# A hybrid token-mixing and expert layer on one core: a written TensorE and ScalarE order up to the end of the u projection

## The chip, the cores and the metric

The kernel runs on one core of one Trainium2 chip. The metric is the device time of one execution in microseconds (us); less is better. A core has TensorE (PE, matrix products; its weight loads are listed as PEld), VectorE (DVE), ScalarE (ACT), GpSimd (POOL) and SyncE (SP), which issues most DMA transfers. Each engine works through its own list of instructions in order, and waits for the others by semaphores.

## The reference

One layer for 512 latent tokens and 256 context tokens, 1024 wide, in float32:

```
mod   = silu(c) @ ada_w + ada_b            # 6 vectors of 1024; the same for c_ctx
h, hc = modulate(rms_norm(x)), modulate(rms_norm(ctx))      # shift 1 and scale 1
q, k, v, r, lr, u = split(h @ w_in)                         # the same for hc
GLA:  log_a = log_sigmoid(lr @ lr_up + bias) / 16; a gated linear scan in both directions
S5:   lam_bar = exp(lam*dt); b_bar = ((lam_bar-1)/lam)*B; a diagonal complex scan of u, both directions
x  = x + g1 * (concat(GLA, S5) @ w_out)
x  = x + g2 * moe(modulate(rms_norm(x)))   # 32 experts, 4 for each token
out = rms_norm(x)
```

## The kernel before, in words

Everything lies in one function, `hybrid_layer_kernel`, and in `moe_phase`, which it calls at the end. The Python code issues operations; a scheduler decides each engine's list from its own model of time, except inside `manual_schedule` blocks, where the named engines keep the order in which the code stands. Tiles come from rings of named slots, and a tile waits until a slot of its ring is free. Those that matter here:

- `place(n)` are 13 single slots of 1 MB; `half(n)` are six of 512 KB, which first hold the six tiles `xt` of x and ctx.
- `whalf(name)` without a number is a ring of three 512 KB slots. It carries t32s, then the four tiles of `wu` (weights of u), the first tile of `wqk` (weights of q and k), the tile vt0, the other three of `wqk`, qT, kT and then `wv` and `wr_`.
- `work(...)` is a ring of four slots of 256 KB, called t2k. It carries, in the order of the code, the scratch of the S5 weights (`wtmp`, L399), the scratch of the output weights (`cd`, L441, also named wtmp in the trace), the copies of u (uT and uTc, L622 to L630), two rows mb (L503) and the temporaries of the gates (ab, abc).
- `bank` is a ring of six PSUM banks, `side` gives one of two more.

The order of the work up to the end of u. SP has a written list of early loads (L166 to L183): four tiles of x, eight of `ada_w` for the first half of the features, `wu`, ctx, B, `wu`, eight more of `ada_w`, C. `turned_tokens` (L229) scales and transposes a tile of tokens; ScalarE's order of this is written (L245). `shifts(p, k)` (L267) multiplies one tile of `ada_w`, `columns(p)` (L276) makes the scale and shift columns A1, B1 from it, and `modulate(p)` (L518) applies them, p being the half of the features. The first half stands before u. For S5, `pick` and two blocks of transposes (L331 to L373) spread the decays and B, and `chunk_weights(d)` (L391) forms for each direction d eight blocks with three VectorE operations, a block of transposes and a ScalarE copy each.

The u projection is 32 units (L577 to L594), four slices h of the features by eight outputs; a unit is two matrix products. TensorE's order of it is written: eight `shifts(1, k)`, `columns(1)` after unit 4, `low_rank` before unit 17 and a step of `condition` (L486) after every second unit from unit 9 (units count from 0). A step of `condition` reads 1 MB of `ada_w` into a ring of two slots and multiplies it; there are 16, for the four other modulation vectors. After the loop, and outside of the written order, stand `chunk_weights(0)` and `(1)`, `output_columns` (L411: the C columns cc), `output_weights` (L424: 16 groups of three VectorE operations for cl), the VectorE work of the long decays lv, the copies of u to DRAM and back, the remaining steps of `condition` and its end. Then follow the gates (L672 to L691), `lags` (L446, reads cl), the projection of q and k (pk, L732 to L739, with `chunk_inputs` after its first slice, which fills vt and XV for the scan), the scan on VectorE, and the projections v (pvv) and r (pr), attention, output projection, norm, router, and the 32 experts, each with 12 MB of weights.

Of the kernel before, what the change touches and what calls it, by code (L numbers as in the profile page):

```python
# [20 lines left out]
D = 1024  # L21
L = 512
# [16 lines left out]
AFTER = (1, 2, 3, 4)  # L39
LOW0 = 7  # L40
LOW1 = 17
COND0 = 9
COND = 2
# [7 lines left out]
def hybrid_layer_kernel(ctx, tc, I, out, tap=None, stage=99):  # L51
# [114 lines left out]
    with tc.manual_schedule(engines={mybir.EngineType.SP}):  # L166
# [13 lines left out]
        for r, cn in enumerate(("s5_c_re", "s5_c_im")):  # L180
            for d in range(2):
                nc.sync.dma_start(crow[r][d * 16:(d + 1) * 16].rearrange("q h c p -> q h (c p)"),
                                  I[cn][0, d].rearrange("(h q) c p -> q h (c p)", h=2))  # L183

    pr = bank("ps_rows")
# [4 lines left out]
    nc.scalar.activation(sg, cols[:, 0:16], AF.Exp, scale=-1.0)  # L190
    V.tensor_scalar(sg, sg, 1.0, None, OP.add)
    V.reciprocal(sg, sg)
    stc = consts.tile([P, KT, 32], F32, name="stc")
    nc.gpsimd.memset(stc, 0.0)
    for j in range(2):
        nc.vector.tensor_tensor(stc[:, :, j], cols[:, 8 * j:8 + 8 * j], sg[:, 8 * j:8 * j + 8], op=OP.mult)
# [26 lines left out]
    def squares(i):  # L223
        sq = work("sq", (P, D), BF)
        ss = small.tile([P, 1], F32, name="ss")
        nc.scalar.activation(sq, xt[i], AF.Square, accum_out=ss)
        return rstd_root(nc, small, ss, D)

    def turned_tokens(i, root):  # L229
        t = xt[i]  # L230
        rs = rstd_inv(nc, small, *root)
        V.tensor_scalar(t, t, rs, None, OP.mult)
        for hh in range(2):
            pb = bank(f"xT{i}{hh}")
# [10 lines left out]
    with tc.manual_schedule(engines={mybir.EngineType.Activation}):  # L245
        decays()
        root = squares(0)
        for i in range(4):
            after = squares(i + 1) if i < 3 else None
            turned_tokens(i, root)  # L250
            root = after
        angles()
        for i in range(4, 6):
            turned_tokens(i, squares(i))

    gates_w = half(0, "gates_w", (P, 768))
    lrs = gates_w[:, 0:256].rearrange("p (k r) -> p k r", k=KT)
    nc.sync.dma_start(lrs, win[:, :, 1536:1568])  # L260
    gw = gates_w[:, 256:768].rearrange("p (z n) -> p z n", z=2)
    nc.gpsimd.memset(gw, 0.0)
    gnw = consts.tile([P, P], F32, name="gnw")
# [3 lines left out]
    def shifts(p, k):  # L267
        if k == 0:
            pa.append(side(f"ps_ada{p}", 0) if p else bank(f"ps_ada{p}"))
        for c in range(2):  # L270
            for hh in range(2):
                q = 2 * c + hh
                nc.tensor.matmul(pa[p][32 * q:32 * q + 32, :256], stc[:, k, :], adac[p][k][:, c, hh * 256:(hh + 1) * 256],
                                 start=(k == 0), stop=(k == KT - 1), skip_group_check=True)

    def columns(p):  # L276
        with tc.high_priority():
            mrow = work("mrow", (P, 256))
            nc.vector.tensor_copy(mrow, pa[p][:, :256])
            pm = side("ps_mod", 0) if p else bank("ps_mod")  # L280
            for b in range(2):
                transpose(pm[:, b * P:(b + 1) * P], mrow[:, b * P:(b + 1) * P])
            pmv = pm[:, :256].rearrange("p (b c h j) -> p c h b j", b=2, c=2, h=2)
# [6 lines left out]
            for j in range(2):  # L290
                a_, b_ = [o[p][:, j].rearrange("p (h b) -> p h b", h=2) for o in (A1, B1)]
                nc.vector.scalar_tensor_tensor(a_, pmv[:, 1, :, :, j], 1.0, col(24), op0=OP.add, op1=OP.add)
                nc.vector.tensor_tensor(a_, a_, col(32), op=OP.mult)
                nc.vector.tensor_tensor(b_, pmv[:, 0, :, :, j], col(16), op=OP.add)

    for k in range(KT):
        shifts(0, k)
    columns(0)
# [3 lines left out]
    for g2 in range(2):  # L302
        nc.gpsimd.dma_start(rows2[0:4].rearrange("t (q g c) -> t g q c", q=4, g=2)[:, g2],
                            I["s5_d"][0, g2 * 256:(g2 + 1) * 256].rearrange("(t q c) -> t q c", t=4, q=4))
    nc.gpsimd.dma_start(rows2[4:8], I["gla_lr_bias"].rearrange("o z (r p) -> (o z r) p", p=P))
    nc.gpsimd.dma_start(rows2[8:12], I["glu_b"].rearrange("o (r p) -> (o r) p", p=P))
    pr2 = side("ps_pq", 1)
    transpose(pr2[:, :NR2], rows2, NR2)
    V.tensor_copy(cols[:, NR:], pr2[:, :NR2])

    lb = [t32("lbr"), t32("lbi")]
    ff = [t32("ffr"), t32("ffi")]
    V.tensor_tensor(sh, sh, sh, op=OP.mult)
    V.tensor_scalar(sh, sh, -2.0, 1.0, OP.mult, OP.add)
    V.tensor_tensor(lb[0], ea, sh, op=OP.mult)
    V.tensor_tensor(lb[1], ea, sn, op=OP.mult)
    den, t0 = t32("den"), t32("t0")
    V.tensor_tensor(den, lamr, lamr, op=OP.mult)
    V.tensor_tensor(t0, lami, lami, op=OP.mult)
    V.tensor_tensor(den, den, t0, op=OP.add)  # L320
    V.reciprocal(den, den)
    V.tensor_scalar(nn, lb[0], -1.0, None, OP.add)
    V.tensor_tensor(ff[0], nn, lamr, op=OP.mult)
    V.tensor_tensor(t0, lb[1], lami, op=OP.mult)
    V.tensor_tensor(ff[0], ff[0], t0, op=OP.add)
    V.tensor_tensor(ff[0], ff[0], den, op=OP.mult)
    V.tensor_tensor(ff[1], lb[1], lamr, op=OP.mult)
    V.tensor_tensor(t0, nn, lami, op=OP.mult)
    V.tensor_tensor(ff[1], ff[1], t0, op=OP.subtract)
    V.tensor_tensor(ff[1], ff[1], den, op=OP.mult)  # L330
    def pick(ps, src):  # L331

        for g2 in range(2):
            sel = ident[:64, :64].rearrange("k (d g n) -> k g d n", d=2, g=2)[:, g2]
            nc.tensor.matmul(ps[g2 * 64:(g2 + 1) * 64], src, sel, start=True, stop=True, skip_group_check=True)

    pq = side("ps_pq", 1)
    for i, t in enumerate(lb + ff):
        pick(pq[:, i * 32:(i + 1) * 32], t)

# [4 lines left out]
    V.tensor_copy(pw[:, :, 1], pq[:, 0:64].rearrange("p (r g) -> p r g", r=2))  # L345
    V.tensor_copy(fz, pq[:, 64:128].rearrange("p (r g) -> p r g", r=2))
# [10 lines left out]
    for n in (1, 2, 4):  # L357
        bb = [pw[:, r, n:n + 1].to_broadcast([P, n, 32]) for r in range(2)]
        cmul(V, [pw[:, r, n + 1:2 * n + 1] for r in range(2)], [pw[:, r, 1:n + 1] for r in range(2)], bb,
             ctmp[:, :n * 32].rearrange("p (k g) -> p k g", g=32))  # L360

    bb_ = [consts.tile([P, 32, 16], F32, name=f"bb{r}") for r in range(2)]
    pb_ = []
    for r in range(2):
# [7 lines left out]
    fb = [fz[:, r].rearrange("p (g o) -> p g o", o=1).to_broadcast([P, 32, 16]) for r in range(2)]  # L372
    cmul(V, bb_, pb_, fb, ctmp.rearrange("p (g c) -> p g c", c=16))  # L373
# [17 lines left out]
    def chunk_weights(d):  # L391
        pr_, pi_ = powers(0, d, d == 1, 0, True), powers(1, d, d == 1, 0, True)
        br_, bi_ = over_powers(bb_[0], d, True), over_powers(bb_[1], d, True)
        wr = [place(3 + 4 * d + r, f"w{'ri'[r]}{d}", (P, 16, 16, 8)) for r in range(2)]
        wt[d] = [place(5 + 4 * d + r, f"wt{d}{r}", (P, 16, P)) for r in range(2)]
        for g in range(0, 16, 4):
            gs = slice(g, g + 4)
            for r, (o, a, b, op) in enumerate(((wr[0], pr_, pi_, OP.subtract), (wr[1], pi_, pr_, OP.add))):
# [4 lines left out]
                pb = side("ps_w", 1)  # L403
                for j in range(4):
                    transpose(pb[:, j * P:(j + 1) * P], o[:, g + j].rearrange("p c k -> p (c k)"))
                nc.scalar.activation(wt[d][r][:, gs].rearrange("p g s -> p (g s)"), pb, AF.Copy)
# [17 lines left out]
    def output_weights():  # L424
        for r in range(2):
            bd.append(whalf(f"bd{r}", (P, 32, 32), n=3 + r))
            nc.gpsimd.memset(bd[r], 0.0)
# [58 lines left out]
    def condition():  # L486
        ring = keep_.tile([P, 2, 2048], F32, name="adb2", tag="xv")
        mob = whalf("mob", (P, 2, 512), n=5)

        def step(g, k):  # L490
            if k == 0:
                pa2.append(side(f"pa2{g}", 0))
            t = ring[:, k % 2]
            nc.sync.dma_start(t, I["ada_w"][0, k * P:(k + 1) * P, 2048 + g * 2048:4096 + g * 2048])
            for q in range(4):
                nc.tensor.matmul(pa2[g][32 * q:32 * q + 32, :], stc[:, k, :], t[:, q * 512:(q + 1) * 512],
# [21 lines left out]
    def modulate(p):  # L518
        with tc.high_priority():
            for kk in range(4):  # L520
                for m, n, src in sides(p):
                    h, a, b = src[:, kk], A1[p][:, m, kk:kk + 1], B1[p][:, m, kk:kk + 1]
                    if (kk + m) % 2:
                        last = nc.scalar.activation(h, h, AF.Identity, bias=b, scale=a)
                    else:
                        V.tensor_scalar(h, h, a, b, OP.mult, OP.add)
        return last
# [9 lines left out]

    modulate(0)
# [35 lines left out]
    ahead["wu", 2] = wcols("wu", 1568, 2)  # L574
    cond, cond_end = condition()
    todo_c = [(g, k) for g in range(2) for k in range(KT)]
    with tc.manual_schedule(engines={mybir.EngineType.PE}):  # L577
        late = list(range(4, KT))
        for k in range(4):
            shifts(1, k)  # L580
        for i, (h, o) in enumerate([(h, o) for h in range(4) for o in (outs if h else outs[0::2] + outs[1::2])]):
            if i == LOW0:
                ahead["wu", 3] = wcols("wu", 1568, 3)
            if i == LOW1:
                low_rank()
            unit(ahead["wu", h][0], h, *o)
            if i >= COND0 and (i - COND0) % COND == 0:
                cond(*todo_c.pop(0))
            if late and i in AFTER:
                shifts(1, late.pop(0))  # L590
                if not late:
                    columns(1)
                    last = modulate(1)
    with tc.issue_after(last.ins):  # L594
# [1310 lines left out]
```

## Time and profile before

| | us |
|---|---|
| median of 3 runs (1537.7 to 1538.61) | 1538.43 |
| the profiled execution, its whole time | 1538.63 |
| span of its trace, first to last instruction | 1536.8 |
| TensorE busy in the span | 1348.4 (88%) |
| VectorE busy | 530.0 (34%) |
| ScalarE busy | 250.5 (16%) |
| GpSimd busy | 169.0 (11%) |

Times within the profile count from the start of the span. The whole time is 1.8 us longer than the span. Busy time of TensorE overlaps from one matrix product to the next, and its ends are modelled, so it is read as occupancy. In a timeline, a row gives start, length, engine, line, operation and operands; in brackets stands how long the engine had been idle before and what ended that.

### The profile page before, as it was taken

The numbers are of one execution on the slowest core, as the hardware profiler recorded it, in microseconds if no ns is written. First come the engines' busy times: TensorE is split into PE (matmuls) and PEld (weight loads), VectorE is DVE, ScalarE is ACT, GpSimd is POOL, SyncE is SP. The second block draws the span as 40 slices with busy tenths as digits, with TensorE's granted clock in tenths as the row PEclk, the third lists the DMA queues.
The fourth block names the chain that finished last, engine by engine and source line by source line (L and its number), as shares of the span: only waits on it lengthen the run. The fifth ranks groups of instructions, "written<-read, shape, count | busy, mean of one in ns | idle before, by whom it ended". The sixth has DMA issues, their size and how long they took to land. (4 is left out here: it accounts for less than half of the span.)

```text
span 1536.8 us, 21011 instructions
## 1 busy us (share of the span) xinstructions
PE 1348.4 (88%) x8122; PEld 546.3 (36%) x8122; DVE 530.0 (34%) x1378; ACT 250.5 (16%) x548; POOL 169.0 (11%) x159
## 2 busy tenths in 40 slices
PE   3796577999796899999999999999999888888985
PEld 2443253458443233333332333332333222222322
DVE  5952737946337113113212221111221122212125
ACT  4112451144222001001000010000010010000013
POOL 2000000000001001121111121111111111111110
PEclk9898698999898999999999999999999999999998
DMA  9474324223725999999999999999999999999993
GB/s 313 138 243 155 84 82 110 68 67 110 281 105 208 393 368 404 409 410 414 411 406 412 415 409 415 404 414 409 414 411 405 408 415 410 410 404 410 413 400 121
DMA packets 104907, 487.18 MB, mean 317 GB/s; under 512 B 24062, under 2 KB 30878, under 8 KB 53584
## 3 DMA queue, kind: packets, MB, share of 16 engines
q1 hardware_dynamic: 89072, 456.95, 74.6%
q0 software_dynamic: 13984, 24.94, 6.0%
q10 hardware_dynamic: 1728, 3.56, 0.6%
q8 instruction: 88, 1.44, 0.4%
q14 instruction: 35, 0.29, 0.1%
HBM read 468.41 MB, written 22.86 MB: 320 GB/s over the span
## 5 line engine op out<-in xcount | busy, mean ns | idle before, releaser
L1568 PE MATMUL pg<-gu,xT 128*64 128x512 f32 x2048 | 480.6, 601 | 34.7 <-DMA gu<-in_exp_w_gu_dram 27.9
L1568 PEld LDWEIGHTS pg<-gu,xT 128*64 128x64 f32 x2048 | 138.8, 137 | 330.5 <-issue 242.4
L1601 PE MATMUL pd<-dn,aT 128*64 128x512 f32 x992 | 222.8, 594 | 12.0 <-DMA dn<-in_exp_w_down_dram 9.6
L1588 DVE TENSOR_SCALAR at<-rest 128x256 f32<-128x256 f32 x32 | 13.6, 425 | 555.9 <-PE rest L1581 307.2
L1589 ACT ACTIVATE sgm<-at 128x256 f32<-128x256 f32 x96 | 39.7, 413 | 700.7 <-DVE at L1588 677.2
L1601 PEld LDWEIGHTS pd<-dn,aT 128*64 128x64 f32 x992 | 68.5, 136 | 145.5 <-issue 113.0
L1536 POOL DMA_INDIRECT xg<-h2d,iu x47 | 50.1, 1065 | 588.1 <-DVE li L1590 328.7
L1581 PE MATMUL rest<-gu,xT 128*32 128x512 f32 x896 | 107.3, 597 | 0.0
L1652 POOL DMA_INDIRECT acc<-y,iu x30 | 47.7, 1589 | 205.0 <-DMA acc<-yr,iu 175.0
L1552 ACT ACTIVATE aT<-turn 128x512 f32<-128x512 f32 x64 | 27.9, 487 | 204.0 <-PE turn L114 204.0
L1652 POOL DMA_INDIRECT acc<-yr,iu x30 | 48.2, 1607 | 56.7 <-DMA acc<-y,iu 32.7
L1650 DVE SCALAR_TENSOR_TENSOR yr<-rest,gt,g2r 128x256 f32<-128x256 f32 x30 | 14.5, 483 | 107.9 <-DMA acc<-yr,iu 73.7
L1611 PE MATMUL rest<-dn,aT 128*32 128x256 f32 x896 | 50.8, 379 | 0.0
L1581 PEld LDWEIGHTS rest<-gu,xT 128*32 128x32 f32 x896 | 24.4, 109 | 69.1 <-issue 67.9
L114 PE MATMUL turn<-ident,at 128*128 128x128 f32 x192 | 32.0, 302 | 9.3 <-PEq L1686 4.7
L549 PE MATMUL pvv<-wv_w,xn 128*128 128x512 f32 x64 | 31.2, 645 | 7.2 <-DMA wv_w<-in_w_in_dram 7.2
L1592 DVE TENSOR_TENSOR at<-at,sgm 128x256 f32<-128x256 f32 x96 | 37.3, 415 | 0.0
L1591 DVE SCALAR_TENSOR_TENSOR at<-li,at 128x256 f32<-128x256 f32 x96 | 37.2, 414 | 0.0
L1450 DVE CAST e<-mt 96x64 bf16<-96x64 f32 x32 | 6.3, 206 | 89.3 <-PEq L1686 46.3
L114 PEld LDWEIGHTS turn<-ident,at 128*128 128x128 f32 x192 | 25.8, 209 | 30.1 <-issue 25.7
L1498 DVE TENSOR_TENSOR ohs<-mt 128x1024 bf16<-128x1024 f32 x30 | 36.5, 1215 | 0.0
L549 PE MATMUL pk<-xn,wqk_w 128*128 128x512 f32 x64 | 31.5, 629 | 3.1 <-DVE la L683 3.1
(550 smaller groups left out, 1429.1 us busy)
## 6 DMA issues: line engine op xcount, KB each, us to landing
gu<-in_exp_w_gu_dram SPq DMA_DIRECT2D x252, 1024.0 KB
dn<-in_exp_w_down_dram SPq DMA_DIRECT2D x128, 1024.0 KB
adb<-in_ada_w_dram SPq DMA_DIRECT2D x16, 1024.0 KB
ada<-in_ada_w_dram SPq DMA_DIRECT2D x16, 512.0 KB
wo<-in_w_out_dram SPq DMA_DIRECT2D x4, 1024.0 KB
gu<-in_exp_w_gu_dram POOLq DMA_DIRECT2D x4, 1024.0 KB, 11.7
xt<-in_x_dram SPq DMA_DIRECT2D x4, 512.0 KB
wu_w<-in_w_in_dram SPq DMA_DIRECT2D x4, 512.0 KB
```

The lines of the kernel that those rows point to most:

```text
L114: nc.tensor.transpose(ps, src, ident[:k, :k])
L549: nc.tensor.matmul(o, lhs(k, w[:, kk]), rhs(k, w[:, kk]), start=opens and k == 0, stop=k == KT - 1, skip_group_check=True)
L1498: V.tensor_tensor(ohs, iot.rearrange("p (o s) r -> p o (s r)", o=1).to_broadcast([P, 4, 2 * P]), pm.to_broadcast([P, 4, 2 * P]), op=OP.is_ ...
L1536: last = nc.gpsimd.indirect_dma_start(out=x[:, c0:c1], out_offset=None, in_=src, in_offset=bass.IndirectOffsetOnAxis(ap=iu[:, s:s + 1], ax ...
L1568: nc.tensor.matmul(pg[b][64 * q:64 * q + 64], xT[:, k % 4, (k // 4) * 64:(k // 4 + 1) * 64], gu[k][:, :, c:c + 256], start=False, stop=(k ...
L1581: nc.tensor.matmul(pr[32 * q:32 * q + 32], xT[:, 4 + k % 2, (k // 2) * 32:(k // 2 + 1) * 32], gu[k][:, :, q * 256:(q + 1) * 256], start=Fa ...
L1589: nc.scalar.activation(sg, at, AF.Sigmoid, scale=1.702)
L1591: V.scalar_tensor_tensor(at, li, 1.0, at, op0=OP.add, op1=OP.mult)
L1592: V.tensor_tensor(at, at, sg, op=OP.mult)
L1601: nc.tensor.matmul(pd[64 * q:64 * q + 64], aT[:, k % 4, (k // 4) * 64:(k // 4 + 1) * 64], dn[k][:, q * 512:(q + 1) * 512], start=False, st ...
L1611: nc.tensor.matmul(pe[32 * q:32 * q + 32, 0:256], aT[:, 4 + k % 2, (k // 2) * 32:(k // 2 + 1) * 32], dn[k][:, q * 256:(q + 1) * 256], star ...
L1652: nc.gpsimd.indirect_dma_start(out=dst, out_offset=bass.IndirectOffsetOnAxis(ap=iu[:, s:s + 1], axis=0), in_=src, in_offset=None, bounds_c ...
```

## The change

From the start up to the last unit of u, both TensorE and ScalarE now keep a written order. In it:

- the squares of a token tile, its scaling and its transposes are separate functions that are called one tile ahead of each other; the eight `shifts(0, k)` stand between them; the units on the latent tokens of slice 0 begin when the first half of the latent features is modulated, and the two context tiles, the S5 pieces (`small_columns`, `picked`, `input_rows`) and the context's modulation stand between the first units;
- `shifts(1, k)` come two at a time after units 7 to 10; `columns(1)` then uses ScalarE for its PSUM copies and GpSimd for its six small operations, and `modulate(1)` is all on ScalarE;
- a step of `condition` follows every unit from 12 until the 16 are done; its ring has four places of 1 MB (two of them in the slots that held x and ctx tiles), filled by two DMAs each;
- the transposes and copies of `chunk_weights` become 16 turns, one after every unit from 14; `low_rank` moves to unit 20, `output_columns` into the loop at unit 23; the VectorE part of `chunk_weights(1)` and the long decays are issued at unit 10;
- `output_weights` moves behind the copies of u in the code; three small loads (gnw, rwt, rbb) move from GpSimd's queue to the end of SP's early list; two memsets of bd and one each of gw and stc move from GpSimd to VectorE;
- vt0, vt1, qT and kT leave the ring `whalf` for slots of their own (whalf 5 and 4, place 10).

The core of the diff:

```
+ADA1 = (7, 8, 9, 10)
+LOW = 20
+OUT = 23
+COND0 = 12
+CHUNK0 = 14
...
+        nc.sync.dma_start(gnw, raw(I["gla_norm_w"], 0, [[0, P], [1, P]]))
+        nc.sync.dma_start(rwt, I["router_w"][0].rearrange("(k p) e -> p k e", p=P))
+        nc.sync.dma_start(rbb, raw(I["router_b"], 0, [[0, P], [1, 32]]))
...
     def columns(p):
+        eng = nc.gpsimd if p else V
         with tc.high_priority():
             mrow = work("mrow", (P, 256))
-            nc.vector.tensor_copy(mrow, pa[p][:, :256])
+            if p:
+                nc.scalar.activation(mrow, pa[p][:, :256], AF.Copy)
+            else:
+                V.tensor_copy(mrow, pa[p][:, :256])
...
+                eng.tensor_tensor(a_, pmv[:, 1, :, :, j], one_more[:, p].rearrange("p (h b) -> p h b", h=2), op=OP.add)
+                eng.tensor_tensor(a_, a_, col(32), op=OP.mult)
+                eng.tensor_tensor(b_, pmv[:, 0, :, :, j], col(16), op=OP.add)
...
     def chunk_weights(d):
...
+        def turn(r, g):
+            pb = side("ps_w", 1)
+            for j in range(4):
+                transpose(pb[:, j * P:(j + 1) * P], wr[r][:, g + j].rearrange("p c k -> p (c k)"))
+            nc.scalar.activation(wt[d][r][:, g:g + 4].rearrange("p g s -> p (g s)"), pb, AF.Copy)
...
+        return [(turn, r, g) for g in range(0, 16, 4) for r in range(2)]
...
     def condition():
-        ring = keep_.tile([P, 2, 2048], F32, name="adb2", tag="xv")
+        ring = keep_.tile([P, 4, 1024], F32, name="adb2", tag="xv")
...
+            n = (g * KT + k) % 4
+            if n < 2:
+                ts = [ring[:, 2 * n + i] for i in range(2)]
+            else:
+                ts = [half(2 * n - 2 + i, "adb3") for i in range(2)]
...
+    with tc.manual_schedule(engines={mybir.EngineType.PE, mybir.EngineType.Activation}):
+        ss = [squares(i) for i in range(2)]
+        transpose(pr[:, :NR], rows, NR)
...
+        scaled_tokens(0, ss[0])
+        scaled_tokens(1, ss[1])
+        turned_tokens(0)
+        ss.append(squares(2))
+        turned_tokens(1)
+        shifts(0, 0)
...
+        scaled_tokens(3, ss[3])
+        turned_tokens(3)
+        for k in range(3, KT):
+            shifts(0, k)
+        angles()
+        discretized()
+        columns(0)
+        modulate(0, (0,))
+        w = [ahead["wu", h][0] for h in range(2)]
+        unit(w[0], 0, *outs[0])
+        small_columns()
+        unit(w[0], 0, *outs[2])
+        picked()
...
+        unit(w[0], 0, *outs[4])
+        input_rows(0)
+        turned_tokens(4)
+        unit(w[0], 0, *outs[6])
+        input_rows(1)
+        input_matrix()
+        turned_tokens(5)
+        modulate(0, (1,))
...
+        turns = chunk_weights(0)
...
+            unit(ahead["wu", h][0], h, *o)
+            if i in ADA1:
+                for k in range(2):
+                    shifts(1, late.pop(0))
                 if not late:
                     columns(1)
+                    modulate(1)
+                    turns += chunk_weights(1)
+                    long_decays()
+            if i == LOW:
+                low_rank()
+            if i == OUT:
+                output_columns()
+            if i >= COND0 and todo_c:
+                cond(*todo_c.pop(0))
+            if i >= CHUNK0 and turns:
+                f, *a = turns.pop(0)
+                f(*a)
...
         nc.sync.dma_start(udc[t * P:(t + 1) * P], uTc.rearrange("p s c -> p (s c)"))
+    for f, *a in turns:
+        f(*a)
+    output_weights()
     for g, k in todo_c:
...
-            vt.append(whalf(f"vt{d}", (P, 16, 2, 32), n=None if d else 5))
+            vt.append(whalf(f"vt{d}", (P, 16, 2, 32), n=5 - d))
...
-    qT, kT = whalf("qT", (P, 2, L)), whalf("kT", (P, 2, L))
+    qk = place(10, "qk", (P, 4, L))
+    qT, kT = qk[:, 0:2], qk[:, 2:4]
```

## Rows read from the trace of the kernel before

**Rows 1.** Stages: window, length, busy us of each engine (instructions), clock, DMA share, GB/s

```profile
0.00:49.10 49.10, 23.11 (x196) 16.90 (x196) 27.50 (x122) 17.98 (x35) 9.62 (x22) 0.99 0.93 288
49.10:61.40 12.30, 12.25 (x52) 4.65 (x52) 12.23 (x15) 2.62 (x5) 0.00 (x0) 0.88 0.61 220
61.40:69.20 7.80, 0.05 (x1) 0.05 (x1) 7.80 (x12) 0.00 (x0) 0.00 (x0) 0.77 0.00 0
69.20:124.90 55.70, 54.93 (x262) 26.48 (x262) 29.79 (x65) 9.97 (x17) 0.00 (x0) 0.97 0.67 223
124.90:147.90 23.00, 16.48 (x208) 10.26 (x200) 3.67 (x7) 7.23 (x13) 0.00 (x0) 0.92 0.43 147
147.90:171.40 23.50, 5.93 (x144) 3.88 (x144) 23.50 (x41) 0.60 (x1) 0.00 (x0) 0.50 0.01 1
171.40:183.40 12.00, 10.09 (x128) 5.42 (x129) 4.01 (x9) 7.42 (x13) 0.99 (x2) 0.86 0.79 214
183.40:212.40 29.00, 18.14 (x121) 11.66 (x119) 19.60 (x42) 25.71 (x39) 0.00 (x0) 0.82 0.38 112
212.40:247.00 34.60, 34.16 (x235) 20.08 (x233) 8.55 (x17) 10.36 (x31) 0.00 (x0) 1.00 0.20 55
247.00:257.50 10.50, 0.79 (x8) 0.45 (x8) 10.50 (x15) 0.46 (x1) 0.00 (x0) 0.64 1.05 265
257.50:329.30 71.80, 71.79 (x161) 31.57 (x162) 57.20 (x117) 6.67 (x10) 0.00 (x0) 0.96 0.15 45
384.00:497.00 113.00, 90.09 (x346) 45.46 (x344) 53.79 (x155) 26.44 (x55) 6.71 (x8) 0.90 0.54 198
497.00:1536.80 1039.80, 956.53 (x5822) 325.26 (x5822) 240.39 (x686) 104.10 (x256) 146.25 (x112) 0.99 0.99 396
```

**Rows 2.** Timeline of VectorE, 144 to 173 us: first and last rows of cl

```profile
144.23 4.91 DVE L442 TENSOR_TENSOR cl<-cc,pw 128x512 f32<-128x512 f32 x8 [45.07 <-ACT cc L418]
...
170.73 2.49 DVE L444 TENSOR_TENSOR cl<-cl,wtmp 128x512 f32<-128x512 f32 x4
```

**Rows 3.** Timeline of ScalarE: the first copy of u and the first row of the gates

```profile
171.44 0.60 ACT L625 ACTIVATE uT<-pu 128x512 f32<-128x512 f32 x1 [22.92 <-DVE cl L444]
...
180.49 0.69 ACT L682 ACTIVATE ab<-pg,cols 128x512 f32<-128x512 f32 x1 [3.93 <-DMA ud<-uT]
```

**Rows 4.** Timelines of TensorE and SP: q and k, their weights, and v

```profile
183.41 1.88 PE L549 MATMUL pk<-xn,wqk_w 128*128 128x512 f32 x4
...
257.51 10.12 PE L549 MATMUL pvv<-wv_w,xn 128*128 128x512 f32 x16 [7.20 <-DMA wv_w<-in_w_in_dram]
...
205.69 15.98 SPq L146 DMA_DIRECT2D wqk_w<-in_w_in_dram x3
```

**Rows 5.** Timelines up to the first unit of u, all engines

```profile
2.98 11.02 SPq L163 DMA_DIRECT2D ada<-in_ada_w_dram  x8
...
22.37 3.68 PE L114 MATMUL xT<-ident,xt 128*128 128x128 f32 x16 [1.94 <-DVE xt L232]
...
23.19 0.75 DVE L232 TENSOR_SCALAR xt<-xt,rs 128x1024 f32<-128x1024 f32 x1
...
42.12 3.66 PE L273 MATMUL ps_ada<-ada,stc 128*32 128x256 f32 x64
...
45.85 0.42 DVE L279 COPY mrow<-ps_ada 128x256 f32<-128x256 f32 x1 [2.91 <-PE ps_ada L273]
...
49.11 5.09 PE L549 MATMUL pu<-xn,wu_w 128*128 128x512 f32 x8 [0.47 <-DVE xn L526]
```

**Rows 6.** Timeline of TensorE in the u loop: starts of two units of the same kind

```profile
104.24 1.98 PE L549 MATMUL pu<-xn,wu_w 128*128 128x512 f32 x4
...
108.45 1.98 PE L549 MATMUL pu<-xn,wu_w 128*128 128x512 f32 x4
```

**Rows 7.** Timeline, 9 to 12 us: a VectorE row and a GpSimd row beside it

```profile
9.86 1.73 DVE L211 TENSOR_SCALAR t32s<-lami,t32s 64x64 f32<-64x64 f32 x1
...
10.54 0.97 POOL L427 MEMSET bd<- 128x1024 f32 x1
```

More of the change, by code (lines that the diff above doesn't have):

```diff
@@ L242, in turned_tokens @@
                 nc.scalar.activation(dst, src, AF.Copy)
[L245 to L263, printed above, removed]
     A1, B1, pa = [], [], []
@@ L323, in hybrid_layer_kernel @@
[L323 to L335, printed above, removed]
@@ L355, in cmul, with pick @@
         eng.tensor_tensor(o[1], o[1], tmp, op=OP.add)
[L357 to L362, printed above, removed]
-    pb_ = []
-    for r in range(2):
+    def pick(ps, src):
+        for g2 in range(2):
+            sel = ident[:64, :64].rearrange("k (d g n) -> k g d n", d=2, g=2)[:, g2]
+            nc.tensor.matmul(ps[g2 * 64:(g2 + 1) * 64], src, sel, start=True, stop=True, skip_group_check=True)
@@ L365, in hybrid_layer_kernel, with input_rows @@
+    def input_rows(r):
         pb = side(f"ps_b{r}", 1)
@@ L573, in hybrid_layer_kernel @@
         outs.append((puc[t // 2][:, (t % 2) * LC:(t % 2 + 1) * LC], t % 2 == 0, colsl(t), lambda k, wk: hctx(k)))
-    ahead["wu", 2] = wcols("wu", 1568, 2)
     cond, cond_end = condition()
     todo_c = [(g, k) for g in range(2) for k in range(KT)]
[L577 to L582, printed above, removed]
+    one_more = consts.tile([P, 2, 4], F32, name="one_more")
@@ new lines, in hybrid_layer_kernel @@
+    with tc.manual_schedule(engines={mybir.EngineType.PE, mybir.EngineType.Activation}):
+        ss = [squares(i) for i in range(2)]
+        transpose(pr[:, :NR], rows, NR)
+        V.tensor_copy(cols[:, :NR], pr[:, :NR])
+        silu()
+        V.tensor_scalar(one_more.rearrange("p a b -> p (a b)"), cols[:, 24:32], 1.0, None, OP.add)
+        decays()
+        scaled_tokens(0, ss[0])
[4 more added lines that the diff above has]
+        shifts(0, 0)
+        scaled_tokens(2, ss[2])
+        ss.append(squares(3))
+        turned_tokens(2)
+        shifts(0, 1)
+        shifts(0, 2)
+        scaled_tokens(3, ss[3])
[11 more added lines that the diff above has]
+        picked()
+        ss += [squares(i) for i in range(4, 6)]
+        for i in range(4, 6):
+            scaled_tokens(i, ss[i])
+        unit(w[0], 0, *outs[4])
[6 more added lines that the diff above has]
+        modulate(0, (1,))
+        gates_w = half(0, "gates_w", (P, 768))
+        lrs = gates_w[:, 0:256].rearrange("p (k r) -> p k r", k=KT)
+        gw = gates_w[:, 256:768].rearrange("p (z n) -> p z n", z=2)
+        V.memset(gw, 0.0)
+        nc.sync.dma_start(lrs, win[:, :, 1536:1568])
+        for q in range(4):
+            for z in range(2):
+                nc.sync.dma_start(gw[q * 32 + z * 16:q * 32 + (z + 1) * 16, z], I["gla_lr_up"][0, z])
+        turns = chunk_weights(0)
+        late = list(range(KT))
+        ahead["wu", 2] = wcols("wu", 1568, 2)
+        for i, (h, o) in list(enumerate([(h, o) for h in range(4) for o in (outs if h else outs[0::2] + outs[1::2])]))[4:]:
+            if i == 8:
```

176 lines of the change are left out of this document (84 added, 92 removed).

## The prediction

> **What bounds the kernel now.** I first cut the span into stages by what TensorE works on, and read each stage's busy times [rows 1]. The last one, the experts, is two thirds of the span; TensorE is busy 957 of 1040 us there and 396 GB/s come in. The change touches nothing in it. In the 113 us ahead of it only 198 GB/s move, half of that, so the experts' weights aren't what that stage waits for: their slots come free as the layer's first part ends. A microsecond saved before it should therefore arrive at the end whole.
>
> The reader should look next at where TensorE idles before 329 us [rows 1]: 7.8 us from 61.4 (VectorE is busy without a break), 6.5 us from 124.9, 17.6 us from 147.9 (VectorE again), 10.9 us from 183.4 and 9.7 us from 247.0. Before 49.1 it is busy for only 23.1.
>
> The chain behind the 147.9 stage starts far ahead of it. VectorE stood idle for 45 us until ScalarE delivered cc, at 144.2, since `output_columns` is behind everything else in TensorE's list; then it made cl in one run until 173.2 [rows 2], 29 us for 16 groups of three operations, 0.61 each. The copies of u waited 22.9 us for it although u had ended at 124.9: their t2k slots were given out behind the scratch of cl. The gates' first row came at 180.5, held by the copies of u [rows 3]. The q and k projection began 2.9 us behind it, at 183.4, as its banks come behind those of the gates. Its other weights were issued only at 205.7, behind vt0 in their ring, and v stood 7.2 us for its own [rows 4].
>
> **The change part by part.** All sums are made against the profiled execution, 1538.63, which is 0.2 above the median of 1538.43.
>
> *First unit of u: from 49.1 to about 32.* Eight tiles of `ada_w` and four of x are 6.3 MB, which at the 288 GB/s of the first stage are in by 21.9 us. Token tile 3 was scaled at 23.9. Behind that, in the new order: its transposes, half of a row that has two tiles, 1.8; five `shifts`, 40 records at 3.66/64 = 0.057, 2.3; and from the copy of the row to the first unit as now, 49.1 - 45.9 = 3.3. That gives 31.3; 32 with some slack for the sine and its copies on ScalarE [rows 5].
>
> *End of u: from 124.9 to about 131.* Everything that TensorE does until 147.9 now lies in one order. Its busy time until then is 23.1 + 12.3 + 0.05 + 54.9 + 16.5 = 106.8 [rows 1]. Ahead of the first unit lie four tiles of transposes (7.4) and 64 records of `shifts` (3.7) [rows 5]; 95.7 are left. New waits: at about five places TensorE stands for a ScalarE copy of 0.60 [rows 3] (the context's transposes, `input_rows`, the row of `columns(1)`, cc), some 3.5. So 32 + 95.7 + 3.5 = 131. u itself ends 6 us later than now, but conditioning, the 16 turns and cc are done with it. The bounds are 126 (no such wait, first unit at 31) and 138 (twice the waits, first unit at 35).
>
> *Does VectorE keep up?* Its work for a direction is 24 operations of `chunk_weights`, in the stage from 61.4 about 0.65 us each (12 in 7.8), so some 2 us a turn [rows 1], and a cycle of TensorE with two units, a turn and a step of conditioning was 4.21 us [rows 6]. With a turn and a step after every unit it will be near 2.9, still above 2, and the first turn stands some 20 us behind the first VectorE operation. I cost that at nothing; should VectorE start 10 us late, the turns would pass on about half of it.
>
> *`columns(1)` through GpSimd and ScalarE.* Its six operations have no row before. Below they cost nothing, since VectorE's queue no longer holds TensorE (the 7.8 us). Above, each stands as long as a row in which VectorE seems to be held by GpSimd: a 64x64 operation that lasted 1.73 and ended with GpSimd's memset beside it [rows 7], so 6 x 1.73 = 10.4. Units 11 to 15 cover about 8.3 of that chain (two cycles of 4.21), of which ScalarE's copies and first modulations take some 3.5; 5.6 would show. I take 0, as the tiles are only 4 wide, and keep 5.6 for the range. The Trainium skill, SBUF — State Buffer, section on the two separate sides, says that VectorE operations with two SBUF inputs and GpSimd operations that read SBUF take a shared port pair in turn, each for a whole instruction. By that rule the six would each wait for one of `chunk_weights`' products, and the upper bound would be the nearer one; no row here has such a pair.
>
> *cl, the copies of u and the gates: about 23 us earlier.* At 131 the copies of u start at once. cc lies some eight units back, so VectorE can make the first product of each group, 16 x 0.61 = 9.8 us, while u still runs. The other 32, 19.5 us, need scratch slots, which the copies of u now hold first; they gave them up within about 7 us (from 171.4 to the gates at 180.5 were 9.1 for all eight) [rows 3]. So cl is ready at 131 + 7 + 19.5 = 157.5 instead of 173.2. The gates' slots come right behind it, at about 157, against 180.5: 23.5 us earlier; q and k begin 2.9 later, at 160 against 183.4 [rows 4]. I take 23.
>
> *Rings.* With vt0, qT and kT out of it, the ring of weights holds nothing but weights, so q and k's are there long before, and v's too. Of the 10.9 us idle from 183.4 I give back 5, because the copies of the scan's inputs on ScalarE and the gates share that time (25.7 of 29 busy); of the 9.7 from 247.0, 8 [rows 1]. The new slots of vt0 and vt1 wait for the end of conditioning and for `lags`, both near 165, when pv is only starting. The bounds are 0 and 20.6.
>
> *Costed at nothing:* the second DMA of each step and the three loads moved to SP, which in the stages up to 147.9 mostly waits; the memsets moved to VectorE, which then idles before cc. If SP were late, the steps of `condition` would be: a rival below.
>
> *Who waits behind the written waits.* A TensorE wait for a turn or a tile of `ada_w` now holds all units behind it; a ScalarE wait for GpSimd's columns holds the copies of the turns.
>
> The sum is -23 - 13 = **-36 us, 1502.6**. VectorE's scan moves along: in the stage of v and r it is idle for 14.6 of 71.8 us [rows 1], so it isn't what ends there.
>
> **The rivals.** *A, as summed.* For it: each released wait has its row.
>
> *B, shift only (1515.6).* The idle stretches from 183.4 and 247.0 stay, as SP's list puts the weights behind another wait, and only the 23 are won. For it: SP issues in order and has waited so at 205.7. Against it: the slots are free earlier.
>
> *C, q and k overtake (1489).* If the banks of q and k no longer stand behind the gates, TensorE works from 138 on through the busy times of what follows until 329.3: 5.9 + 10.1 + 18.1 + 34.2 + 0.8 + 71.8 = 140.9, that is until 279 instead of 329.3 [rows 1], -50. Against it: they began behind the gates' last one now.
>
> *D, slower (1543).* Conditioning now stands between nearly all units from 12 to 27, so TensorE cannot end u before 16.8 MB are in. They can start once the last token tile is transposed, at about 50. At the 223 GB/s of the stage from 69.2 they end at 125, with 7 us of units behind them: no loss. At the 147 GB/s of the stage from 124.9 u ends at 50 + 114 + 7 = 171, 40 later than summed, and the kernel is 4 us slower: 1543. It decides from 167, that is 153 GB/s. Against it: the lower rate was seen with two places and TensorE's turns between; now there are four.
>
> *E, no change (1538.6).* The experts' stream doesn't start earlier, because its slots or SP's list hang on something else. Against it: 198 GB/s ahead of it.
>
> **How the numbers follow.** A has 0.53, B 0.20, C 0.15, D 0.07, E 0.05. The predicted time is A's. Its own bounds: end of u by -5 and +7, the rings by -7 and +13, GpSimd by +5.6. The range, 1484 to 1526, takes in C with 5 us more, and B with u at 138 (1522.6) and most of GpSimd's share; D, E and the outer tails are left out. About 0.2% (3 us) is what a measurement can tell from no change. Faster: A, B and C, 0.88; same: E, 0.05; slower: D, 0.07.
>
> **What would show it.** The first unit of u near 32; the last at 126 to 138 with cc ahead of it; uT right behind it; the last cl near 157; the gates' first row near 157, q and k's first product near 160; no wait of v for its weights; the experts' first product near 461 instead of 497. The prediction is wrong if TensorE shows long waits for adb, wr or A1 within u, if uT again stands behind cl, or if the stage of the gates grows by what was won before.

## The result and the profile after

The changed kernel takes 1517.39 us (median; 1514.96 to 1520.75), the kernel before beside it 1538.52: a ratio of 0.9864, 95% interval 0.9843 to 0.9884, some 21 us less. The forecast was 1502.6 in a range of 1484 to 1526: the direction is right and the time lies in the range, but of the 36 us summed only 21 came. The profiled execution has a span of 1514.7 us, 22.1 less than before.

The stages by what TensorE works on, as in [rows 1], of the kernel after (columns as there):

```profile
30.00:64.00 34.00, 30.98 (x173) 17.60 (x173) 27.42 (x63) 10.46 (x19) 0.00 (x0) 0.85 0.90 295
64.00:77.40 13.40, 0.00 (x1) 0.00 (x0) 13.40 (x22) 0.38 (x1) 0.00 (x0) 0.63 0.02 6
77.40:90.70 13.30, 13.27 (x58) 5.75 (x58) 13.30 (x24) 0.38 (x1) 12.07 (x1) 0.86 0.47 145
90.70:98.00 7.30, 0.02 (x4) 0.00 (x0) 3.44 (x16) 5.37 (x9) 2.01 (x6) 0.79 0.95 372
98.00:155.00 57.00, 55.57 (x388) 27.74 (x388) 9.25 (x17) 14.73 (x26) 0.00 (x0) 0.91 0.57 191
155.00:181.80 26.80, 12.94 (x266) 8.29 (x265) 23.89 (x41) 6.72 (x12) 1.05 (x2) 0.68 0.29 72
181.80:234.80 53.00, 49.06 (x359) 30.06 (x353) 21.36 (x52) 29.77 (x60) 0.00 (x0) 0.97 0.18 60
475.00:1514.70 1039.70, 955.24 (x5823) 324.15 (x5822) 240.94 (x687) 104.75 (x257) 146.04 (x112) 0.99 0.99 396
```

Read from below. The experts' stage is as long as before (1039.7 against 1039.8), so everything was won ahead of it. The projection of q and k with the scan's inputs takes 53.0 us, where [rows 4] have 74.1 between pk and pvv: that is 21.1 of the 22.1. Its start moved by only 1.6 (181.8 against 183.4). So the start of q and k, which was to come 23 us earlier through the reordered first part, hardly moved; and the table shows why: within u TensorE stands still twice, for 13.4 and for 7.3 us. The first unit did start early, at 30.06 (forecast 32, before 49.1), and u ended at 155 (forecast 131, before 124.9).

What the two holes wait for stands in the timelines of TensorE and ScalarE after:

```profile
77.44 0.69 PE L115 MATMUL ps_mod<-ident,mrow 128*128 128x128 f32 x2 [13.43 <-ACT mrow L282]
...
98.02 1.11 PE L115 MATMUL ps_w<-ident,wi 128*128 128x128 f32 x4 [7.29 <-ACT wt L422]
...
77.00 0.38 ACT L282 ACTIVATE mrow<-ps_ada 128x256 f32<-128x256 f32 x1 [17.29 <-DVE wr L430]
...
92.59 0.81 ACT L555 ACTIVATE xn<-xn,B,A 128x512 f32<-128x512 f32 x1 [14.05 <-POOL A L302]
```

The first is a slot: mrow, the row from which `columns(1)` makes its columns, is a t2k tile, and the ring's four slots are out with `chunk_weights`' scratch; ScalarE waits 17.29 us until VectorE has used one up (wr), and TensorE's list stands behind mrow's transposes. The kernel before waited for the same row, in the 7.8 us from 61.4 of [rows 1]. VectorE copied it there, behind its products; the first row below is TensorE's, the other two are VectorE's of the kernel after:

```profile
69.15 0.69 PE L114 MATMUL ps_mod<-ident,mrow 128*128 128x128 f32 x2 [7.79 <-DVE mrow L279]
...
72.25 3.85 DVE L429 TENSOR_TENSOR wtmp<-bb,pw 128x512 f32<-128x512 f32 x4
...
76.19 0.71 DVE L430 TENSOR_TENSOR wr<-wr,wtmp 128x512 f32<-128x512 f32 x1
```

In the code before, `columns(1)` stood ahead of `chunk_weights(0)`, and mrow ahead of its scratch in the ring. Now `chunk_weights(0)` is called first, and mrow comes behind its eight scratch tiles. Four of these are in use until the first four sums, the other four are filled from 72.25 on; mrow gets the slot that the fifth sum gives up (76.19 + 0.71 = 76.90), and its copy starts at 77.00.

The second begins on GpSimd, whose whole work between 30 and 155 us is this:

```profile
78.63 13.33 POOL L301 TENSOR_TENSOR A<-pms,one_more 128x4 f32<-128x4 f32 x1 [72.97 <-ACT pms L290]
91.93 0.18 POOL L303 TENSOR_TENSOR B<-pms,cols 128x4 f32<-128x4 f32 x1
92.08 0.19 POOL L301 TENSOR_TENSOR A<-pms,one_more 128x4 f32<-128x4 f32 x1
92.22 0.18 POOL L303 TENSOR_TENSOR B<-pms,cols 128x4 f32<-128x4 f32 x1
92.37 0.34 POOL L302 TENSOR_TENSOR A<-A,cols 128x4 f32<-128x4 f32 x2
```

Of two operations of the same form and size one lasts 13.33 us and the other 0.19. ScalarE, which has the modulation next in its written order, waits 14.05, and the copies of the turns (wt) stand behind it.

The order of the later steps is the forecast one (ScalarE's and VectorE's timelines, against [rows 2, 3]):

```profile
155.18 0.61 ACT L693 ACTIVATE uTc<-puc 128x256 f32<-128x256 f32 x1 [2.04 <-PE puc L577]
...
176.59 0.69 ACT L750 ACTIVATE ab<-pg,cols 128x512 f32<-128x512 f32 x1 [19.85 <-DVE cl L469]
...
150.81 4.91 DVE L467 TENSOR_TENSOR cl<-cc,pw 128x512 f32<-128x512 f32 x8 [3.90 <-PE ps_w L115]
...
160.16 2.50 DVE L468 TENSOR_TENSOR wtmp<-cc,pw 128x512 f32<-128x512 f32 x4 [1.66 <-DMA ud<-uT]
```

The copies of u no longer stand behind cl; cl's scratch now waits for them, and the gates for cl. From the end of u to the gates' first row pass 21 us, 26 were summed.

### The profile page after: what moved, and what is told of

Same layout as the page of the kernel before. It is cut to its first block, busy times and chain, and to the rows that moved or that the text cites. A ratio compares the mean times of both kernels' runs of the same rounds, so it can differ in the third digit from the quotient of the medians.

```text
span 1514.7 us, 21032 instructions
## 1 busy us (share of the span) xinstructions
PE 1345.6 (89%) x8123; PEld 544.4 (36%) x8123; DVE 529.8 (35%) x1373; ACT 251.1 (17%) x552; POOL 178.1 (12%) x158
## 5 line engine op out<-in xcount | busy, mean ns | idle before, releaser
L577 PE MATMUL pu<-xn,wu_w 128*128 128x512 f32 x64 | 35.7, 686 | 1.2 <-issue 1.2
L115 PE MATMUL turn<-ident,xg 128*128 128x128 f32 x192 | 28.1, 284 | 6.9 <-PEq L1746 5.5
```

The source lines that it names most:

```text
L115: nc.tensor.transpose(ps, src, ident[:k, :k])
L577: nc.tensor.matmul(o, lhs(k, w[:, kk]), rhs(k, w[:, kk]), start=opens and k == 0, stop=k == KT - 1, skip_group_check=True)
```

## The experiments

All ratios are to the kernel before, run on the same chip beside the variant.

### Which half of the change gives the time

**r1_rings_only**, the kernel before with the new slots alone:

```
-            vt.append(whalf(f"vt{d}", (P, 16, 2, 32), n=None if d else 5))
+            vt.append(whalf(f"vt{d}", (P, 16, 2, 32), n=5 - d))
...
-    qT, kT = whalf("qT", (P, 2, L)), whalf("kT", (P, 2, L))
+    qk = place(10, "qk", (P, 4, L))
+    qT, kT = qk[:, 0:2], qk[:, 2:4]
```

> The kernel before with one thing alone from the change's tail: vt0, vt1, qT and kT leave the ring of weights as they do after the change; no written order, no turns between units, two conditioning places. Theory 'rings': the 21 us that the change won all come from here, since after the change the stretch from q and k's first product to v's was 53.0 us instead of 74.1, and q and k itself began only 1.6 us earlier. Then this kernel takes 1517 (1513 to 1522), v doesn't wait for wv_w, and q and k begin at 183 as before. Theory 'order' (the prediction's: the earlier end of cl and gates gives most): at most 13 us are won here, 1525 or more.

Measured: 1526.36 us, on a chip on which the kernel before took 1541.32: 0.9901 (0.9880 to 0.9922), 15 us less (12 to 19 by the interval). v waits for no weights. The profiled execution tells more than the time. These are TensorE's rows of the first product of q and k, of the first of v, and of a step of conditioning ahead of both; the last row is such a step in the kernel before:

```profile
189.49 13.04 PE L549 MATMUL pk<-xn,wqk_w 128*128 128x512 f32 x30
...
244.81 11.32 PE L549 MATMUL pvv<-wv_w,xn 128*128 128x512 f32 x26
...
132.85 1.94 PE L496 MATMUL pa<-adb,stc 128*32 128x512 f32 x8 [1.45 <-DMA adb<-in_ada_w_dram]
...
131.85 1.06 PE L496 MATMUL pa<-adb,stc 128*32 128x512 f32 x8
```

The stretch from pk to pvv is 55.3 us, 18.8 shorter than before, but it begins 6.1 us later. TensorE's granted clock was 0.50, the lower of its two levels, from 132.8 to 145.3 us, where the kernel before had 0.95, and eight products pa took 1.94 us instead of 1.06. Ahead of that row TensorE had waited 1.45 us for adb; but the kernel before has such a wait too (1.63 at 127.58), so why the clock fell here stays open, and whether r1's other runs had it is not known.

**o1_order_only**, the changed kernel with vt0, qT and kT back in the ring of weights:

```
-            vt.append(whalf(f"vt{d}", (P, 16, 2, 32), n=5 - d))
+            vt.append(whalf(f"vt{d}", (P, 16, 2, 32), n=None if d else 5))
...
-    qk = place(10, "qk", (P, 4, L))
-    qT, kT = qk[:, 0:2], qk[:, 2:4]
+    qT, kT = whalf("qT", (P, 2, L)), whalf("kT", (P, 2, L))
```

> The changed kernel with vt0, qT and kT put back into the ring of weights, as before the change; the written order, the turns between units and the four places stay. Theory 'rings': q and k begin at about 182 as after the change, v waits for its weights again, and only 0 to 4 us of the 21 are left: 1534 to 1538. Theory 'order': 1522 or less.

Measured: 0.9956 (0.9941 to 0.9972), 7 us less; q and k begin at 185.0, v at 253.2 after a wait of 5.0 for its weights:

```profile
253.24 9.65 PE L577 MATMUL pvv<-wv_w,xn 128*128 128x512 f32 x16 [5.00 <-DMA wv_w<-in_w_in_dram]
```

The two halves add up to the change (15 and 7 against 21), and neither theory holds to the letter. "Rings" wanted all 21 from the slots and at most 4 from the rest. "Order" wanted at most 13 from the slots, which r1's interval does not exclude, but then this kernel at 1522 or less, and it took 1533.49. By the times the rings give about two thirds, the order one third. The stretch from pk to pvv divides alike: 74.1 us before, 68.2 here, 53.0 in the changed kernel, so 5.9 of its 21.1 come from the order and 15.2 from the slots.

**r2_vt_only**, r1 without its second edit:

> The kernel before with vt0 and vt1 in their new slots, qT and kT still in the ring of weights. Theory 'vt0 alone holds the ring': as r1_rings_only, ratio 0.990. Theory 'qT and kT hold v's weights': q and k begin and end as there, but v still waits some 7 us for wv_w, whose slots come behind qT and kT: ratio 0.994 to 0.997.

Measured: 0.9885 (0.9860 to 0.9909), no different from r1; v's first product waits 1.02 us for its weights, so the second theory is out. It was vt0 that held the ring; moving qT and kT is not seen in the time.

### The two holes within u

**m1_mrow_own**, the changed kernel with the row in memory that is there anyway (pms, written only once the transposes have read the row):

```
-            mrow = work("mrow", (P, 256))
+            pms = consts.tile([P, 256], F32, name="pms") if p else None
+            mrow = pms if p else work("mrow", (P, 256))
...
-                pms = consts.tile([P, 256], F32, name="pms")
```

> The changed kernel, with the row mrow of columns(1) in pms's own memory instead of a slot of the scratch ring that it takes behind the scratch of chunk_weights. TensorE's wait of 13.4 us for mrow goes; the row is copied near 64 instead of 77. Theory 'held by VectorE' (GpSimd's first small operation lasts until the products of chunk_weights end, whenever it started): it starts near 65 and lasts some 27 us, to 92, the wait moves to the turns and the u that need its columns, and the time falls by 0 to 5: 1512 to 1517. Theory 'first operation' (the 13.3 us are a fixed price of GpSimd's first arithmetic): it still lasts 13 us, to 78, and the time falls by about 13: 1504.

Measured: 0.9849 (0.9822 to 0.9875), its six times from 1507 to 1521; by the ratio alone it can't be told from the changed kernel. The profiled run is the fastest of the six. The wait for mrow is gone, and TensorE waits 12.44 for wt instead of 7.29. GpSimd's list in m1, and VectorE's rows beside its first two ends:

```profile
64.83 1.25 POOL L301 TENSOR_TENSOR A<-pms,one_more 128x4 f32<-128x4 f32 x1 [59.15 <-ACT pms L290]
66.04 6.41 POOL L303 TENSOR_TENSOR B<-pms,cols 128x4 f32<-128x4 f32 x1
72.40 3.98 POOL L301 TENSOR_TENSOR A<-pms,one_more 128x4 f32<-128x4 f32 x1
76.34 0.19 POOL L303 TENSOR_TENSOR B<-pms,cols 128x4 f32<-128x4 f32 x1
76.49 6.45 POOL L302 TENSOR_TENSOR A<-A,cols 128x4 f32<-128x4 f32 x2
...
65.92 0.20 DVE L321 TENSOR_TENSOR ctmp<-lv 128x32 f32<-128x32 f32 x1
66.04 3.91 DVE L428 TENSOR_TENSOR wi<-bb,pw 128x512 f32<-128x512 f32 x4
...
72.28 0.21 DVE L322 TENSOR_TENSOR lv<-lv,ctmp 128x32 f32<-128x32 f32 x1
```

Both theories fall as they were put: there is no fixed price of a first operation (it took 1.25), and none waits to the last product. The time came where the first theory had it, as the wait moved to the turns. Each long one ends where VectorE, between its 128x512 operations, runs a small one of `long_decays`: 64.83 + 1.25 = 66.08 lies in the row from 65.92 to 66.12, 66.04 + 6.41 = 72.45 in that from 72.28 to 72.49.

**m2_no_breaks** takes these small rows out of the train, to test that:

```
-                    long_decays()
+                    with tc.issue_after(ends[-1].ins):
+                        long_decays()
```

(`ends` collects the third operation of each group of `chunk_weights`.)

> As m1_mrow_own, with the small VectorE operations of long_decays (128x32) all behind the last product of chunk_weights instead of among them. In m1 the GpSimd operations, started at 64.8, ended at 66.1, 72.4, 76.4 and 82.9, each within 0.2 us of one of those small VectorE operations; in the changed kernel the first one ended at 92.0, as the products did. Theory 'held by VectorE's train' (GpSimd gets its operands only where the 128x512 products are broken): now the first GpSimd operation, started near 65, lasts until the last product, near 90, some 25 us, and the six are done at 91; the time stands near the changed kernel's, ratio 0.986 to 0.990. Rival 'a turn now and then' (GpSimd gets through after some products, whatever they are): the six end near 83 as in m1, in steps of 1 to 7 us; ratio 0.982 to 0.986.

Measured: 0.9871 (0.9855 to 0.9887), and TensorE waits 21.42 us for wt. GpSimd's first rows in m2, and VectorE's train, its last sum and what follows:

```profile
68.01 25.79 POOL L301 TENSOR_TENSOR A<-pms,one_more 128x4 f32<-128x4 f32 x1 [62.35 <-ACT pms L290]
93.77 0.18 POOL L303 TENSOR_TENSOR B<-pms,cols 128x4 f32<-128x4 f32 x1
...
68.80 3.91 DVE L429 TENSOR_TENSOR wi<-bb,pw 128x512 f32<-128x512 f32 x4
...
92.94 0.69 DVE L431 TENSOR_TENSOR wi<-wi,wtmp 128x512 f32<-128x512 f32 x1
93.54 0.19 DVE L386 COPY lv<-pw 128x64 f32<-128x64 f32 x1
```

One 128x4 operation of GpSimd stands 25.79 us and ends at 93.80, just behind the last of 32 128x512 operations that VectorE, from 68.80 on, makes without a break, each with two inputs in SBUF. The lengths of GpSimd's rows are rough, but ScalarE agrees: it stood 26.51 us for A. The theory has its number, and the rival ("a turn now and then") is out.

**a1_columns_scalar** takes GpSimd out of the chain and leaves mrow as it is:

```
-                eng.tensor_tensor(a_, pmv[:, 1, :, :, j], one_more[:, p].rearrange("p (h b) -> p h b", h=2), op=OP.add)
...
+                        nc.scalar.activation(A1[p][:, :, i], pmv[:, 1, h, b, 0:2], AF.Identity, bias=om_w[:, p, i:i + 1],
+                                             scale=cols[:, 32 + 4 * p + i:33 + 4 * p + i])
+                        nc.scalar.activation(B1[p][:, :, i], pmv[:, 0, h, b, 0:2], AF.Identity,
+                                             bias=cols[:, 16 + 4 * p + i:17 + 4 * p + i])
```

> The changed kernel with the six GpSimd operations of columns(1) written as eight ScalarE activations (one VectorE product of two 1x8 rows early, for the bias). Both theories of the 13.3 us GpSimd operation want the same here: the eight take some 0.3 us each, the modulation of the second half starts near 81 instead of 92, and TensorE's wait of 7.3 us for ScalarE's wt goes; the wait of 13.4 us for mrow stays. Time about 7 less than the changed kernel, 1510 (1506 to 1517). If the time doesn't fall, the end of u isn't what the later stages hang on.

Measured: 0.9800 (0.9783 to 0.9816). The eight operations take 80.46 to 82.43, the second hole is gone and the first stays (14.24).

**v1_columns_vector** is m1 with `eng = V` for both halves:

> As m1_mrow_own, with the six small operations of columns(1) on VectorE, as before the change, instead of GpSimd. In VectorE's list they stand behind the first four sums of chunk_weights, four of them there and two one group of products later, so they should run near 72 and 77. Theory 'GpSimd was the dear place': each takes about 0.2 us there, ScalarE modulates from about 77 on instead of 79 to 83 in m1, TensorE's wait for wt shrinks, u ends near 138: ratio 0.976 to 0.980, between am_both and m1. Rival 'VectorE's list holds it as before the change': they come only behind all products, near 92, ratio 0.985 or more.

Measured: 0.9768 (0.9745 to 0.9792). The first four run at 72.87 to 73.23, 0.14 each, the last two at 77.19; ScalarE modulates from 77.38, and TensorE waits 6.61 for wt. So once mrow has memory of its own, the six operations are cheaper on VectorE, where the kernel before had them too (0.15 each), than on GpSimd: 0.9768 against m1's 0.9849.

**am_both** joins m1 and a1:

> Both repairs in the changed kernel: mrow in pms's memory, and the columns of the second half on ScalarE. Theory 'whole': the 13.4 and the 7.3 us add up and everything behind u moves with its end: last unit near 134 instead of 155, the gates' first row near 156, q and k near 161, the experts' first product near 455; about 20 less than the changed kernel, ratio to the kernel before 0.973 (0.970 to 0.977). Theory 'overlap': the single repairs gave less than their waits (about 5 and 10 by the times) and the second hides part of the first: ratio 0.978 to 0.983.

Measured: 0.9728 (0.9707 to 0.9749), 1496.55 us. Rows of ScalarE (end of u, gates) and TensorE (q and k, experts):

```profile
132.04 0.62 ACT L704 ACTIVATE uTc<-puc 128x256 f32<-128x256 f32 x1 [2.04 <-PE puc L586]
...
153.38 0.69 ACT L761 ACTIVATE ab<-pg,cols 128x512 f32<-128x512 f32 x1 [19.77 <-DVE cl L478]
...
158.59 0.70 PE L586 MATMUL pk<-xn,wqk_w 128*128 128x512 f32 x1
...
455.01 4.83 PE L1648 MATMUL pg<-gu,xT 128*64 128x512 f32 x16 [0.31 <-issue]
```

u ends 23.1 us earlier than in the changed kernel (132.0 against 155.1), the gates begin 23.2 earlier, q and k 23.2, the experts 20.5. So 'whole' holds: the holes don't overlap, and here a microsecond of u reaches the end nearly whole. The single repairs gave less, as m1 alone only moves the wait to GpSimd.

### The places of the conditioning ring, and cl

**c2_two_places** is the changed kernel, **b2_two_places** is b1 (below), each with

```
-            n = (g * KT + k) % 4
+            n = (g * KT + k) % 2
```

> The changed kernel with conditioning's tiles in two places (the old memory) instead of four; order and rings as changed. Theory 'supply': a step behind every unit wants 1 MB every 2.9 us, two places can't bring that, TensorE stands for adb within u, u ends 10 to 20 later and half or all of the change's 21 us is lost: ratio 0.992 to 1.0. Theory 'places don't matter': the loads keep ahead of the steps anyway: ratio 0.985 to 0.988 as with four.

Measured: 0.9878 (0.9858 to 0.9898), not to be told from the changed kernel. TensorE waits for adb eleven times, 7.1 us in all, but part of that lies where the changed kernel waits for wt, which is 1.77 here instead of 7.29; ScalarE's modulation, for which wt stands, also began earlier (90.16 instead of 92.59). u ends at 155.59, as in the changed kernel (155.18).

> b1_early_out with conditioning's tiles in two places. In the changed kernel two places cost TensorE 7.1 us of waiting for adb in eleven pieces, but the time moved by less than its interval, as the wait for GpSimd's columns was shorter in that run. Here nothing else holds u. Theory 'places count once u runs free': u ends 7 to 15 later and the ratio rises from 0.965 to 0.970 to 0.975. Theory 'places don't matter': 0.963 to 0.967.

Measured: 0.9688 (0.9671 to 0.9705) against 0.9649 of b1 (0.9625 to 0.9672): about 6 us in the time, a little under the first theory's bounds; the two intervals just touch. The trace has the rest: 7.4 us of waits for adb, u ends 12.8 us later than in b1 (147.89 against 135.07), and q and k begin 9.3 later (157.23 against 147.91). The four places are worth some 6 us, once nothing else holds u.

**b1_early_out** goes on from am_both:

```
-OUT = 23
+OUT = 18
...
-            if i >= CHUNK0 and turns:
-                f, *a = turns.pop(0)
-                f(*a)
+            for _ in range(1 if i < OUT else 2):
+                if i >= CHUNK0 and turns:
+                    f, *a = turns.pop(0)
+                    f(*a)
...
+    output_weights()
     Us = [place(11 + j, f"U{j}") for j in range(2)]
...
     for f, *a in turns:
         f(*a)
-    output_weights()
```

> As am_both, with the products cl taken into u as well: output_columns behind unit 18 instead of 23, from there two turns behind a unit instead of one, and output_weights written ahead of the copies of u, so that cl's scratch comes first. Theory 'cl holds the gates': the 22 us from u's end to the gates' first row are cl's second half; VectorE stands idle from about 92 until cc now, cl would end near 128 within u, and the gates start some 4 us behind u: 15 less than am_both, ratio about 0.963. Theory 'something else holds them' (u's round through DRAM to U, lags, conditioning's rows): cl ends early but q and k and what follows start as in am_both, 0 to 5 less.

Measured: 0.9649 (0.9625 to 0.9672), 1484.49 us, the fastest here. VectorE's last rows of cl, ScalarE's first of the gates and TensorE's of q and k and of the experts:

```profile
129.42 1.31 DVE L478 TENSOR_TENSOR cl<-cl,wtmp 128x512 f32<-128x512 f32 x2
...
143.24 0.69 ACT L762 ACTIVATE ab<-pg,cols 128x512 f32<-128x512 f32 x1 [6.62 <-DMA ud<-uT]
...
147.91 1.55 PE L586 MATMUL pk<-xn,wqk_w 128*128 128x512 f32 x3
...
442.00 5.29 PE L1649 MATMUL pg<-gu,xT 128*64 128x512 f32 x16 [0.31 <-issue]
```

cl ends within u, and the gates begin 10.1 us earlier than in am_both, although u ends 3.0 later (135.07); 12 arrive at the end, where 15 were expected. They now wait for a slot that u's copy gives up by DMA.

**after_again**, the changed kernel once more:

> The changed kernel once more, to stand beside the others on one chip. Both theories: ratio 0.984 to 0.989. The first GpSimd operation of columns(1), begun near 79, ends at one of VectorE's small operations or with the last product, by 92 at the latest; the time of a run goes with it.

Measured: 0.9873 (0.9850 to 0.9896). Its first GpSimd operation, begun at 82.05, ended at 86.09, in a small VectorE row that began at 86.06; the five others lasted to 95.4. Whether the time of a run goes with this, one profiled run does not show.

## Why the prediction was right and wrong

- **First unit of u**, forecast 32: 30.06. Right.
- **End of u**, forecast 131 between 126 and 138: 155.1. This is where the sum broke, by 24 us, and the runs put 23.1 of them on the two holes: with both mended, u ends at 132.0. The holes themselves are 13.4 and 7.3 us. The rest lies in the products: for the same 619 of them from the first unit to the end of u, TensorE was busy for 99.9 us in the changed kernel, at a granted clock of 0.85, and for 96.1 in am_both, at 0.92. The counting of TensorE's busy time (95.7) and of the short waits (3.5; am_both has 4.7 idle) was right. Two other steps were not:
  - *VectorE keeps up, costed at nothing.* The rate was a little off: 2 us a turn by the mean of one stage, where a product of `chunk_weights` starts every 0.96 us and a sum every 0.60, 2.5 a turn, and where all sixteen products wr and wi of both directions stand ahead of the first sum. But no turn waited for VectorE; am_both, with the same turns, has no such wait. What failed is a wait that the sum doesn't have: ScalarE stood 17.29 us, and TensorE 13.43, for the slot of mrow, a tile of the same t2k ring as the scratch, behind which the change had put it. The forecast took the 7.8 us of [rows 1] as gone because VectorE no longer makes the copy; the copy went to ScalarE and waited longer. m1 shows that the slot is the whole of this wait.
  - *`columns(1)` through GpSimd: 0, at most 5.6.* The upper bound gave each of the six 1.73 us, the length of one row of another pair. The first alone measured 13.33 (7.3 showing on TensorE), and 25.79 in m2. The Trainium skill, SBUF — State Buffer, section on the two separate sides, has whoever starts first keep the shared port pair for a whole instruction, and the other blocked. m2 agrees that the two get in each other's way; that GpSimd gets its turn behind one instruction, as the forecast read the rule, is not what m2 shows, where it stood behind 32.

  The forecast had named its own sign of failing, long waits for adb, wr or A1 within u. The second hole is one: ScalarE stood 14.05 us for A, and TensorE behind it.
- **cl, the copies of u and the gates, 23 us earlier**: 3.9 (176.59 against 180.49). The order of the steps was right (u, its copies, the rest of cl, the gates: 21 us where 26 were summed), the start was late. In am_both the step gives 27.1 (153.38): 157 were forecast for the gates and 160 for q and k, 153.4 and 158.6 were measured.
- **Rings, 13 us between 0 and 20.6**: r1 alone measured 15 (12 to 19), so the term was about right or a little small; the stretch from pk to pvv is 18.8 shorter by r1 and 15.2 by o1. In the changed kernel it is 21.1 shorter, with the 5.9 of the order. Of these, 4.0 are busy time of TensorE (53.09 against 49.06, at a granted clock of 0.97 instead of 0.88), which the forecast had not counted, and 17.1 idle time. The reason given, vt0 in the ring, is shown by r2; that qT and kT mattered is not.
- **The rivals.** B's time (1515.6) is close to the measured one, but by the opposite way: the shift was missing and the rings came. C: q and k still began behind the gates, 5.2 us after their first row (2.9 before). D: conditioning's loads held nothing with four places; with two, TensorE waited 7.1 (c2) and 7.4 us (b2) for them, which cost time only in b2, about 6. E: the experts began 21.5 us earlier (475.49).

That the time lay in the range is in good part luck: one term was too large by 19 us (23 against 3.9), and the stretch from pk to pvv gave 8 more than its term (21.1 against 13).

## What to carry to other kernels

A written order makes every operand of the ordered engines a gate: go through it operand by operand, ask which ring each tile comes from and who holds its slots at that moment, a row of 128x256 like mrow no less than a big tile. A small operation is not free because it is small: moved to GpSimd beside a train of two-input VectorE operations it waited here for a break in the train (25.79 us in m2), and on VectorE itself, in the right place of its list, it took 0.14 us. And where a change mixes a reordering with new slots, measure each alone before believing the sum.

## What the runs showed of the hardware that was not expected

- GpSimd's 128x4 operation with SBUF operands lasts 0.18 or 0.19 us with VectorE in small operations or idle, and 25.79 us in m2 beside unbroken 128x512 operations of VectorE with two SBUF inputs. In m1, m2, after_again and the changed kernel it got in only at VectorE's small operations, and not at every one: in the changed kernel's profile, where it took 13.33, it missed those near 82, 85 and 89 us, in after_again it took the one at 86.06. What decides that stays open. In the rows the next VectorE operation starts before the one ahead ends (0.60 from start to start, 0.68 long), but that holds for the small ones too, so it doesn't explain the difference.
- A VectorE product of two broadcast operands, 128x512, started every 0.96 us for wr and wi and every 0.60 for cl, as plain sums do. They differ in the innermost dimension (8 and 16 elements) and in the steps with which pw is read; no run takes the two apart.
